# Squares of x moved ahead of two evictions, and single buffers for three of eight weight quads, in a hybrid decoder block

## The chip, the core and the metric

The kernel runs on one core of one Trainium2 chip. The metric is the time of one execution on the device in microseconds. The work is spread over TensorE (PE, the matmuls), VectorE (DVE), ScalarE (ACT), GpSimd (POOL) and SyncE (SP, which only issues DMAs here); ACT and POOL issue DMAs too. Each engine works through its own queue in order.

## The reference

One decoder layer on x of 512 tokens by 2048 channels, in float32. What matters here:

```python
u = _rmsnorm(h, norm_w)                       # h is x
proj = jnp.matmul(u, w_in)                    # 2048 x 20528
# split: mLSTM q, k, v, o, z, i, f; DeltaNet q, k, v, z, b, a; gate_a, gate_b
h_a = ... # mLSTM in chunks, per-head RMSNorm, * sigmoid(o) * silu(z)
h_b = ... # conv + silu on q, k, v, gated delta rule in chunks, RMSNorm, * silu(z)
y = sigmoid(gate_a) * (h_a @ w_out[:2048]) + sigmoid(gate_b) * (h_b @ w_out[2048:])
out = _rmsnorm(h + y, final_norm_w)
```

with `_rmsnorm(x, w) = x * rsqrt(mean(x*x) + 1e-6) * w`.

## The kernel before

**Split products.** Every large matmul is done in a reduced format in three passes. Each operand is split into a rounded part, which ACT casts (`split_hi`, L141), and the rest, which DVE subtracts (`split_lo`, L144). The passes are high by high, low by high and high by low. Weights come from DRAM through SP into `wr` tiles (4 buffers), are split into `wh` and `wl` tiles (4 buffers each, pool `wp`), and are then used by PE.

**Order of the work.** PE's order is the program's. All other engines are ordered when the program is built, by a scheduler that walks a simulated timeline and takes, on each engine, the ready instruction of the highest priority. `high_priority(offset=n)` and `urgent(level)` raise a priority (`urgent(3)` by three times `PRIO`, the weight preparation by two times), and `issue_after` puts an instruction behind a named one on its engine. On the chip each engine then keeps that order, and an instruction that has to wait holds all that stand behind it.

**The first block.** `u` is held transposed in 16 column tiles of 128 channels (k tiles, `KT` = 16), high part `uh` and low part `ul`. The load of x is in six pieces `xts[0..5]` (L270), four of 256 columns and two of 512; between them four weight tiles are loaded (`load_raw`, after pieces 0, 1, 3 and 5). The first product (`proj_cm(ML_Q, before=first_block, after=rescale)`) starts before the token factors of the norm are known:

- `make_u(kt)` turns a k tile of x with four PE transposes (L332) into PSUM; ACT writes `uh` (L333) and DVE writes `ul` (L334). These are the evictions. `first_block(kt)` calls `make_u(kt + 2)`, and two k tiles' products follow each two calls.
- The first eight k tiles (`KU` = 8) are not yet scaled by the token factor. The factor needs the sums of squares of all 2048 columns: `squares(n)` (ACT L300 for two of the four token groups, DVE L296 for the other two) for n = 0 to 5, of which 4 and 5 are the two wide pieces, called at kt = 5.
- `token_factors()` adds the sums (L303, L304), and POOL takes the power -0.5 (L305). Then `scale_x(4)`, `factor_row()` (`diag`, L318) and `scale_x(5)` follow, which scale the last 1024 columns of x before they are turned (L311, L313).
- At kt = 6 (`KU - KP`) PE multiplies ones by `diag` (`turn_row`, L324), and ACT copies the result to `rrow` (L325), the row of factors. `rescale` multiplies the half-done products by it (L396), and `scale_u` repairs the first eight k tiles of u (L341, L342).

**The seven-product blocks.** 13 blocks of the input projection (L630 to L632, `seven`) and two of the output projection compute a 512 by 1024 result by seven products of half size instead of eight. A block has a first part A of eight weight quads with four products each (m6, m1, m5, m7) and a second part B of eight quads with three products each (m1, m5, m7). B goes on in the PSUM banks of A's m1, m5 and m7; so before B's first product on a bank DVE must have added what A left there (`add`, L684, at `urgent(3)`) to `U1` or `C22`.

A quad is three weight tiles in one `wr3` tile (3 buffers). For a quad of part A, DVE computes a pair of differences (L572) and one sum `ts` (L573), and POOL stores `ts` to DRAM (L586). For a quad of part B the third tile is that stored `ts` (`t_d`, in the output blocks `t2o_d`), and DVE computes `ts = r0 - r2` (L590), which is split into single buffers `wh`, `wl`; the other two tiles, the pair, are split in one go into the wide buffers `w2h`, `w2l` (128x1024, two buffers each). Part A takes two singles and one wide buffer for each quad, part B one single and one wide buffer. `prep_sums(n + 1)` and `prep_pair(n + 1)` prepare the next quad while quad n is multiplied, `load_quad` then asks for one three ahead. All this preparation is at twice `PRIO`.

Of the kernel before, what the change touches and what calls it, by code (L numbers as in the profile page):

```python
# [8 lines left out]
F32 = mybir.dt.float32  # L9
F32R = mybir.dt.float32r  # L10
AF = mybir.ActivationFunctionType
ALU = mybir.AluOpType
# [9 lines left out]
KP = 2  # L22
# [7 lines left out]
KU = 8  # L30
HP = S // 2
KH = KT // 2
# [27 lines left out]
def hybrid_body(  # L60
# [18 lines left out]
    V, A, G, T = nc.vector, nc.scalar, nc.gpsimd, nc.tensor  # L79
# [22 lines left out]
    normc = cp.tile([P, 33], F32, tag="normc", name="normc")  # L102
# [9 lines left out]
    def load_params(tp):  # L112
        nr = tp.tile([17, P], F32, tag="prow2", name="nrow2")
        nc.sync.dma_start(nr[0:16, :], ml_norm_w.rearrange("(a p) -> a p", p=P))
        nc.sync.dma_start(nr[16:17, :], dn_norm_w.rearrange("(a p) -> a p", p=P))
        cv = dn_conv_w.rearrange("j (a p) -> (j a) p", p=P)
        crs = []
        for i in range(2):
            cr = tp.tile([96, P], F32, tag="crow", name=f"crow{i}", bufs=2)
            nc.sync.dma_start(cr, cv[i * 96:(i + 1) * 96, :])  # L120
            crs.append(cr)
        o = 0
        for ap, n in ((ml_i_bias, MLH), (ml_f_bias, MLH), (dn_a_log, DNH), (dn_dt_bias, DNH)):
            nc.sync.dma_start(bia[:, o:o + n], ap.partition_broadcast(P))
            o += n
        return crs, nr

    def turn_taps(crs, nr, psp):
        pt = psp.tile([P, 256], F32, tag="wk", name="pprt")
        T.transpose(pt[:, 192:209], nr, ident[0:17, 0:17])  # L130
        for i in range(2):
            T.transpose(pt[:, 96 * i:96 * i + 96], crs[i], ident[0:96, 0:96])
        V.tensor_scalar(out=convc, in0=pt[:, 0:192], scalar1=0.5, scalar2=None, op0=ALU.mult)
        V.tensor_scalar(out=normc[:, 16:32], in0=pt[:, 192:208], scalar1=0.125, scalar2=None, op0=ALU.mult)
        V.tensor_scalar(out=normc[:, 32:33], in0=pt[:, 208:209], scalar1=0.25, scalar2=None, op0=ALU.mult)
# [4 lines left out]
    def split_hi(hi, src):  # L140
        newest["A"] = A.copy(hi, src).ins  # L141

    def split_lo(lo, src, hi):
        newest["V"] = V.tensor_tensor(out=lo, in0=src, in1=hi.bitcast(F32), op=ALU.subtract).ins  # L144
# [20 lines left out]
    def load_raw():  # L165
        kind, c, k = plan[len(raws)]
        if kind == "i":
            src, nk, n = w_in[k * P:(k + KP) * P, c:c + NB], KP, NB
        else:
            src, nk, n = w_out[k * P:(k + 1) * P, c:c + NO], 1, NO  # L170
        with tc.high_priority(offset=2 * PRIO if len(raws) > RAHEAD else 0):
            raw = wp.tile([P, nk, n], F32, tag="wr", name="wr", bufs=NRAW)
            newest["S"] = nc.sync.dma_start(raw, src.rearrange("(k p) n -> p k n", p=P)).ins
        raws.append((raw, nk, n))
# [24 lines left out]
    def urgent(level=1):  # L199
        return tc.high_priority(offset=level * PRIO)  # L200
# [25 lines left out]
    uh = up.tile([P, KT, S], F32R, tag="uh", name="uh")  # L226
    ul = up.tile([P, KT * S + 120], F32R, tag="ul", name="ul")[:, 0:KT * S].rearrange("p (k s) -> p k s", s=S)
# [37 lines left out]
    XW = [NB] * (KU // KP) + [2 * NB] * ((KT - KU) // (2 * KP))  # L265
    xts, xat = [], []
    for n, w in enumerate(XW):
        xt = p0.tile([P, NC, w], F32, tag=f"x{n}", name=f"xt{n}")
        o = sum(XW[:n])
        nc.sync.dma_start(xt, xv[:, :, o:o + w])  # L270
        xts.append(xt)
        xat += [(xt, a) for a in range(0, w, P)]
        if n in (0, 1, 3, 5):
            load_raw()
    wg = p0.tile([P, KT, 48], F32, tag="wg", name="wg")
    wgp = p0.tile([P, KT, 112], F32R, tag="wgp", name="wgp")
# [7 lines left out]
    ss = p0.tile([P, NC, len(XW)], F32, tag="ss", name="ss")  # L284
# [1 line left out]
    rrow = p0.tile([P, S], F32, tag="rrow", name="rrow")  # L286
    half = cp.tile([P, 2, NC], F32, tag="half", name="half")
    G.memset(half, 0.5)
    done = {}

    def squares(n):
        w = XW[n]
        for c in range(NC):
            if c % 2:
                jv = p0.tile([P, 2 * NB], F32, tag="jv", name="jv")
                V.scalar_tensor_tensor(out=jv[:, 0:w], in0=xts[n][:, c, :], scalar=1.0, in1=xts[n][:, c, :], op0=ALU.mult,  # L296
                                       op1=ALU.mult, accum_out=ss[:, c, n:n + 1])
            else:
                jk = p0.tile([P, 2 * NB], F32, tag="jk", name="jk")
                A.activation(jk[:, 0:w], xts[n][:, c, :], AF.Square, accum_out=ss[:, c, n:n + 1])  # L300

    def token_factors():
        V.reduce_sum(out=rs, in_=ss, axis=mybir.AxisListType.X)  # L303
        V.tensor_scalar(out=rs, in0=rs, scalar1=1.0 / D, scalar2=EPS, op0=ALU.mult, op1=ALU.add)  # L304
        G.tensor_tensor(out=rs, in0=rs, in1=mhalf, op=ALU.pow)  # L305

    def scale_x(n):
        for c in range(NC):
            xc = xts[n][:, c, :]
            if c % 2:  # L310
                V.tensor_scalar(out=xc, in0=xc, scalar1=rs[:, c:c + 1], scalar2=None, op0=ALU.mult)  # L311
            else:
                A.mul(xc, xc, rs[:, c:c + 1])  # L313

    def factor_row():
        diag = p0.tile([P, NC, P], F32, tag="diag", name="diag")
        for c in range(NC):
            V.tensor_scalar(out=diag[:, c, :], in0=ident, scalar1=rs[:, c:c + 1], scalar2=None, op0=ALU.mult)  # L318
        return diag

    def turn_row(diag):
        pr = psj.tile([P, S], F32, tag="pj", name="prow")
        for c in range(NC):
            T.matmul(pr[:, c * P:(c + 1) * P], ones, diag[:, c, :], start=True, stop=True)  # L324
        A.copy(rrow, pr)  # L325

    def make_u(kt):
        pool, tg = ((psw, "wk"), (pso, "o"))[kt % 2]
        pt = pool.tile([P, S], F32, tag=tg, name="put")
        xt, a = xat[kt]  # L330
        for c in range(NC):
            T.transpose(pt[:, c * P:(c + 1) * P], xt[:, c, a:a + P], ident)  # L332
        done["A"] = A.activation(uh[:, kt, :], pt, AF.Copy, scale=normc[:, kt:kt + 1]).ins  # L333
        done["V"] = V.scalar_tensor_tensor(out=ul[:, kt, :], in0=pt, scalar=normc[:, kt:kt + 1],  # L334
                                           in1=uh[:, kt, :].bitcast(F32), op0=ALU.mult, op1=ALU.subtract).ins

    def scale_u(kt):
        uf = p0.tile([P, KP, S], F32, tag="uf", name="uf", bufs=2)
# [10 lines left out]
    for kt in range(UA):  # L349
        make_u(kt)  # L350
    squares(0)
    gps = {}
# [9 lines left out]
    def first_block(kt):  # L362
        if kt == 3:
            nc.sync.dma_start(wg[:, :, 0:16], w_in[:, ML_I:ML_I + 16].rearrange("(k p) n -> p k n", p=P))
            nc.sync.dma_start(wg[:, :, 16:48], w_in[:, DN_B:DN_B + 32].rearrange("(k p) n -> p k n", p=P))
        if kt == 5:
            taps.extend(load_params(p0))
        if kt == 8:
            with tc.issue_after(done["A"]):
                split_hi(wgh, wg)  # L370
            with tc.issue_after(done["V"]):
                split_lo(wgl, wg, wgh)
        if kt == 12:
            turn_taps(*taps, psw)
        if kt == KU - KP:
            turn_row(gps["diag"])
        if kt + UA < KT:
            make_u(kt + UA)
        if kt % KP and kt < 6:
            squares((kt + 1) // KP)  # L380
        if kt == 5:
            squares(4)
            squares(5)
            token_factors()
            scale_x(4)
            gps["diag"] = factor_row()
            scale_x(5)
        if kt >= KU + 1 and kt % KP:
            scale_u(kt - KU - 1)
        if kt >= KU + GLAG:  # L390
            gate_products(kt - KU - GLAG)
# [141 lines left out]
    def seven_stage(sbp, su, s4, X, t2_d, w_, k0, blocks, sinks, hook, queue):  # L533
# [4 lines left out]
        quads = [(kind, c1, c2, b, g, i) for b, (kind, c1, c2) in enumerate(blocks)  # L538
                 for g in "AB" for i in range(KH)]
# [20 lines left out]
        def split(src, wide):  # L560
            if wide:
                hi, lo = (sbp.tile([P, 2, NO], F32R, tag=f"w2{n}", name=f"w{n}", bufs=2) for n in "hl")
            else:
                hi, lo = (wp.tile([P, 1, NO], F32R, tag=f"w{n}", name=f"w{n}", bufs=NSPL) for n in "hl")
            split_hi(hi, src)
            split_lo(lo, src, hi)
            return [(hi[:, n, :], lo[:, n, :]) for n in range(2 if wide else 1)]
# [25 lines left out]
        def prep_pair(q):  # L593
            if q < len(quads):
                p_, pair = partq[q]
                with tc.high_priority(offset=2 * PRIO):
                    w2 = split(pair, True)
                partq[q] = p_ + w2 if quads[q][4] == "A" else w2 + p_

        JW, OO = ((psj, "pj"), (psw, "wk")), ((pso, "o"),) * 2  # L600
# [1217 lines left out]
```

## Time and profile before

| | before |
|---|---|
| median of three runs | 2182.06 us (2180.47 to 2186.43) |
| the profiled execution | 2178.64 us, of which the span is 2176.4 us |
| mean granted TensorE clock | 0.995 |
| DMA traffic | 444.20 MB, mean 204 GB/s |

The span runs from the first to the last instruction of the program; the time of an execution holds about 2 us more. In the profile's lines an instruction is named by its engine, its line in the kernel, its operation, and `out<-in`; where a wait stands in brackets, it gives the idle time of the engine just before the instruction and what ended it. `PEq`, `SPq` and the like are the engines' sequencers, which issue DMAs. A row of the stretches' table gives for each engine the busy time and the number of instructions, then the granted clock, the share of the DMA engines and GB/s.

### The profile page before, as it was taken

Reading aid. Unit: us, or ns where it says so; the run is one execution under the profiler, and the core shown is the slowest. Engines: PE = TensorE matmul, PEld = TensorE weight load, DVE = VectorE, ACT = ScalarE, POOL = GpSimd, SP = SyncE. Lnnn points to the kernel's source line nnn. Section 1 sums busy time; section 2 is a strip of 40 time slices with the busy share of each in tenths; the row PEclk is TensorE's granted clock in tenths of the full one; section 3 lists DMA queues with packets and bytes.
Section 4 is the critical chain, followed back from the end, with each engine's and each line's share of the span. In section 5 each row is a group of like instructions: output and inputs, shape, how many; then the busy total and the mean of one; then the engine's idle time right before and its main releaser. Section 6 shows DMA issues by size and latency. Waiting matters only on the chain. (4 is left out here: it accounts for less than half of the span.)

```text
span 2176.4 us, 31987 instructions
## 1 busy us (share of the span) xinstructions
PE 2139.7 (98%) x10552; PEld 1763.3 (81%) x10552; DVE 1726.9 (79%) x3001; ACT 1039.2 (48%) x2015; POOL 430.4 (20%) x649
## 2 busy tenths in 40 slices
PE   8999999999999999999999999999999999999998
PEld 6888888878788887888878888888888888877876
DVE  7888798888788778777756887887787888568787
ACT  5444444444444444444445545556455554344345
POOL 0000000000004000000003335235233253242211
PEclk9999999999999999999999999999999999999999
DMA  5456676667568766766867767677687678687885
GB/s 165 122 182 202 193 212 201 216 193 230 188 220 252 237 193 219 242 203 208 266 189 177 189 175 190 160 179 196 174 215 175 161 189 216 197 242 245 248 278 228
DMA packets 449159, 444.20 MB, mean 204 GB/s; under 512 B 197089, under 2 KB 305858, under 8 KB 448866
## 3 DMA queue, kind: packets, MB, share of 16 engines
q1 hardware_dynamic: 379634, 337.22, 53.9%
q0 software_dynamic: 24752, 72.90, 11.0%
q10 hardware_dynamic: 44608, 32.06, 4.7%
q8 instruction: 82, 1.34, 0.3%
q14 instruction: 83, 0.68, 0.1%
HBM read 348.66 MB, written 97.58 MB: 205 GB/s over the span
## 5 line engine op out<-in xcount | busy, mean ns | idle before, releaser
L141 ACT CAST wh<-wr 128x512 fp32r<-128x512 f32 (+1 forms) x522 | 373.3, 716 | 418.8 <-PE pj L252 226.2
L144 DVE TENSOR_TENSOR wl<-wr,wh 128x512 fp32r<-128x512 f32 (+1 forms) x522 | 435.5, 837 | 99.5 <-ACT wh L141 97.2
L251 PE MATMUL pj<-uh,wh 128*128 128x512 f32 x896 | 376.8, 421 | 0.6 <-DVE pj L396 0.5
L253 PE MATMUL pj<-uh,wl 128*128 128x512 f32 x896 | 351.4, 392 | 0.6 <-DVE wl L144 0.6
L252 PE MATMUL pj<-ul,wh 128*128 128x512 f32 x896 | 350.7, 391 | 0.0
L630 PE MATMUL ps<-wh,uh 128*128 128x512 f32 x752 | 295.1, 392 | 8.1 <-DVE X L684 7.6
L631 PE MATMUL ps<-wl,uh 128*128 128x512 f32 x752 | 295.5, 393 | 3.5 <-DVE wl L144 3.2
L632 PE MATMUL ps<-wh,ul 128*128 128x512 f32 x752 | 293.7, 391 | 0.0
L141 ACT CAST wh<-ts 128x512 fp32r<-128x512 f32 x240 | 148.1, 617 | 247.6 <-DVE ts L590 184.4
L141 ACT CAST wh<-t 128x1024 fp32r<-128x1024 f32 x120 | 126.4, 1053 | 276.3 <-PE ps L632 151.6
L630 PE MATMUL ps<-wh,suh 128*128 128x512 f32 x624 | 243.1, 390 | 1.5 <-ACT to L695 1.4
L631 PE MATMUL ps<-wl,suh 128*128 128x512 f32 x624 | 242.8, 389 | 0.0
L632 PE MATMUL ps<-wh,sul 128*128 128x512 f32 x624 | 242.8, 389 | 0.0
L586 POOL DMA_DIRECT2D t_d<-ts x104 | 56.7, 545 | 938.6 <-DVE ts L573 887.5
L253 PEld LDWEIGHTS pj<-uh,wl 128*128 128x128 f32 x896 | 168.4, 188 | 38.5 <-DVE wl L144 1.2
L251 PEld LDWEIGHTS pj<-uh,wh 128*128 128x128 f32 x896 | 169.5, 189 | 31.4 <-DVE pj L396 1.0
L252 PEld LDWEIGHTS pj<-ul,wh 128*128 128x128 f32 x896 | 169.5, 189 | 28.2
L144 DVE TENSOR_TENSOR wl<-ts,wh 128x512 fp32r<-128x512 f32 x240 | 164.0, 686 | 35.5 <-ACT wh L141 35.5
L144 DVE TENSOR_TENSOR wl<-t,wh 128x1024 fp32r<-128x1024 f32 x120 | 146.9, 1224 | 56.5 <-ACT wh L141 55.9
L630 PEld LDWEIGHTS ps<-wh,uh 128*128 128x128 f32 x752 | 141.8, 189 | 42.4 <-DVE X L684 11.8
L631 PEld LDWEIGHTS ps<-wl,uh 128*128 128x128 f32 x752 | 141.9, 189 | 39.0 <-DVE wl L144 10.4
L632 PEld LDWEIGHTS ps<-wh,ul 128*128 128x128 f32 x752 | 141.7, 188 | 28.9
(344 smaller groups left out, 3800.8 us busy)
## 6 DMA issues: line engine op xcount, KB each, us to landing
wr<-in_w_in_dram SPq DMA_DIRECT2D x744, 256.0 KB, 3.7
wr<-in_w_out_dram SPq DMA_DIRECT2D x138, 256.0 KB, 4.9
t_d<-ts POOLq DMA_DIRECT2D x104, 256.0 KB, 4.1
wr<-t_d SPq DMA_DIRECT2D x104, 256.0 KB, 3.9
tg_d<-X ACTq DMA_DIRECT2D x16, 256.0 KB, 6.6
tg_d<-to ACTq DMA_DIRECT2D x16, 256.0 KB, 6.5
v<-v_d SPq DMA_DIRECT2D x8, 512.0 KB, 5.7
mg<-g_d SPq DMA_DIRECT2D x16, 256.0 KB, 4.0
```

What stands on the lines that cost most here:

```text
L141: newest["A"] = A.copy(hi, src).ins
L144: newest["V"] = V.tensor_tensor(out=lo, in0=src, in1=hi.bitcast(F32), op=ALU.subtract).ins
L251: T.matmul(ps[j], hi[:, k, wsl], uh[:, kt, :], start=(kt == 0), stop=False, skip_group_check=after is not None)
L252: T.matmul(ps[j], hi[:, k, wsl], ul[:, kt, :], start=False, stop=False, skip_group_check=after is not None)
L253: T.matmul(ps[j], lo[:, k, wsl], uh[:, kt, :], start=False, stop=(kt == KT - 1 or (after is not None and kt == KU - 1)), skip_group_check= ...
L586: queue.dma_start(t2_d[b % 2, i], ts[:, 0, :])
L630: T.matmul(ps[t], ah, hi, start=(g == "A" and i == 0), stop=False, skip_group_check=True)
L631: T.matmul(ps[t], ah, lo, start=False, stop=False, skip_group_check=True)
L632: T.matmul(ps[t], al, hi, start=False, stop=(i == KH - 1), skip_group_check=True)
```

## The change

There are two edits.

The first is in the first block. The third weight load moves behind x's fifth piece. The squares of pieces 3, 4 and 5 are called at kt = 4, at `urgent(3)`, and before `make_u(6)`; the two evictions of k tile 6 are tied behind the last square on their engine, and those of k tile 7 follow them. The token factors, `scale_x` and `factor_row` at kt = 5 also run at `urgent(3)`.

The second is in `prep_pair`. In part B the pairs of quads 1, 3 and 5 (odd and below `KH - 1` = 7) are split tile by tile into the single buffers `wh`, `wl`, two casts and two subtractions of 128x512 instead of one each of 128x1024. Quads 0, 2, 4, 6 and 7 keep the wide buffers.

```diff
-        if n in (0, 1, 3, 5):
+        if n in (0, 1, 4, 5):
             load_raw()
...
-    done = {}
+    sq, done = {}, {}
...
     def squares(n):
...
-                V.scalar_tensor_tensor(out=jv[:, 0:w], ...)
+                sq["V"] = V.scalar_tensor_tensor(out=jv[:, 0:w], ...).ins
...
-                A.activation(jk[:, 0:w], xts[n][:, c, :], AF.Square, accum_out=ss[:, c, n:n + 1])
+                sq["A"] = A.activation(jk[:, 0:w], xts[n][:, c, :], AF.Square, accum_out=ss[:, c, n:n + 1]).ins
...
     def make_u(kt):
...
-        done["A"] = A.activation(uh[:, kt, :], pt, AF.Copy, scale=normc[:, kt:kt + 1]).ins
-        done["V"] = V.scalar_tensor_tensor(out=ul[:, kt, :], ...).ins
+        with tc.issue_after(sq["A"]) if kt == KU - KP else ExitStack():
+            done["A"] = A.activation(uh[:, kt, :], pt, AF.Copy, scale=normc[:, kt:kt + 1]).ins
+        with tc.issue_after(sq["V"]) if kt == KU - KP else ExitStack():
+            done["V"] = V.scalar_tensor_tensor(out=ul[:, kt, :], ...).ins
...
     def first_block(kt):
...
+        if kt == KU - 2 * KP:
+            with urgent(3):
+                for n in range(3, len(XW)):
+                    squares(n)
         if kt + UA < KT:
             make_u(kt + UA)
-        if kt % KP and kt < 6:
+        if kt % KP and kt < 4:
             squares((kt + 1) // KP)
         if kt == 5:
-            squares(4)
-            squares(5)
-            token_factors()
-            scale_x(4)
-            gps["diag"] = factor_row()
-            scale_x(5)
+            with urgent(3):
+                token_factors()
+                scale_x(4)
+                gps["diag"] = factor_row()
+                scale_x(5)
...
         def prep_pair(q):
             if q < len(quads):
                 p_, pair = partq[q]
+                _, _, _, _, g, i = quads[q]
                 with tc.high_priority(offset=2 * PRIO):
-                    w2 = split(pair, True)
+                    if g == "B" and i % 2 and i < KH - 1:
+                        w2 = split(pair[:, 0:1, :], False) + split(pair[:, 1:2, :], False)
+                    else:
+                        w2 = split(pair, True)
                 partq[q] = p_ + w2 if quads[q][4] == "A" else w2 + p_
```

More of the change, by code (lines that the diff above doesn't have):

```diff
@@ L295, in squares @@
                 jv = p0.tile([P, 2 * NB], F32, tag="jv", name="jv")
-                V.scalar_tensor_tensor(out=jv[:, 0:w], in0=xts[n][:, c, :], scalar=1.0, in1=xts[n][:, c, :], op0=ALU.mult,
-                                       op1=ALU.mult, accum_out=ss[:, c, n:n + 1])
+                sq["V"] = V.scalar_tensor_tensor(out=jv[:, 0:w], in0=xts[n][:, c, :], scalar=1.0, in1=xts[n][:, c, :], op0=ALU.mult,
+                                                 op1=ALU.mult, accum_out=ss[:, c, n:n + 1]).ins
             else:
                 jk = p0.tile([P, 2 * NB], F32, tag="jk", name="jk")
-                A.activation(jk[:, 0:w], xts[n][:, c, :], AF.Square, accum_out=ss[:, c, n:n + 1])
+                sq["A"] = A.activation(jk[:, 0:w], xts[n][:, c, :], AF.Square, accum_out=ss[:, c, n:n + 1]).ins
     def token_factors():
@@ L332, in make_u @@
             T.transpose(pt[:, c * P:(c + 1) * P], xt[:, c, a:a + P], ident)
-        done["A"] = A.activation(uh[:, kt, :], pt, AF.Copy, scale=normc[:, kt:kt + 1]).ins
-        done["V"] = V.scalar_tensor_tensor(out=ul[:, kt, :], in0=pt, scalar=normc[:, kt:kt + 1],
-                                           in1=uh[:, kt, :].bitcast(F32), op0=ALU.mult, op1=ALU.subtract).ins
+        with tc.issue_after(sq["A"]) if kt == KU - KP else ExitStack():
+            done["A"] = A.activation(uh[:, kt, :], pt, AF.Copy, scale=normc[:, kt:kt + 1]).ins
+        with tc.issue_after(sq["V"]) if kt == KU - KP else ExitStack():
+            done["V"] = V.scalar_tensor_tensor(out=ul[:, kt, :], in0=pt, scalar=normc[:, kt:kt + 1],
+                                               in1=uh[:, kt, :].bitcast(F32), op0=ALU.mult, op1=ALU.subtract).ins
     def scale_u(kt):
```

## The prediction

> **What bounds the kernel now.** I read the page first, then the list of waits of PE, then the stretches around each wait, then the timeline there.
>
> ```profile
> span 2176.4 us, 31987 instructions
> PE 2139.7 (98%) x10552; PEld 1763.3 (81%) x10552; DVE 1726.9 (79%) x3001; ACT 1039.2 (48%) x2015; POOL 430.4 (20%) x649
> ```
>
> PE is busy for all but 36.7 us of the span. A change that leaves the matmuls alone, as this one does, can only gain from those microseconds and from stretches in which the busy PE runs slowly. The waits of PE say who holds it (total, times, longest, in us):
>
> ```profile
> PE ps L630 <- DVE X L684: 7.6, 8, 1.8
> PE prow L324 <- DVE diag L318: 3.5, 1, 3.5
> PE ps L631 <- DVE wl L144: 3.2, 5, 1.0
> ```
>
> The second line is the wait that the first edit aims at, the first and third are those that the second edit can reach: B's first products waiting for DVE's `add`, and products waiting for a late low part. The stretches show what such a wait costs beyond itself (columns: PE, PEld, DVE, ACT, POOL busy and counts, granted clock, DMA share, GB/s):
>
> ```profile
> 19.69:23.10 3.41, 0.49 (x3) 0.07 (x1) 2.15 (x8) 1.08 (x2) 1.03 (x1) 0.99 0.55 119
> 23.10:26.51 3.41, 2.86 (x13) 2.86 (x14) 2.58 (x9) 3.12 (x6) 0.00 (x0) 0.50 0.52 134
> 26.51:29.93 3.42, 3.42 (x12) 2.84 (x11) 1.72 (x3) 2.15 (x4) 0.00 (x0) 0.51 0.81 259
> 555.49:558.90 3.41, 1.61 (x7) 1.05 (x6) 2.60 (x5) 1.57 (x2) 0.00 (x0) 1.00 0.27 88
> 558.90:562.32 3.42, 3.42 (x10) 2.64 (x9) 3.42 (x6) 1.47 (x2) 0.00 (x0) 0.51 0.01 2
> 2006.20:2009.60 3.40, 1.88 (x9) 1.47 (x9) 3.13 (x6) 1.57 (x2) 0.00 (x0) 1.00 0.44 159
> 2091.50:2094.90 3.40, 3.40 (x9) 2.66 (x9) 3.40 (x6) 1.93 (x3) 0.00 (x0) 0.50 0.10 36
> ```
>
> A stretch of 3.4 us with PE busy for 0.49 or 1.61 us is followed by one at half clock; one with 1.88 us busy kept the full clock. So a wait of about 1.7 us that falls inside one such stretch costs another 1.7 us, half of the next 3.4; the long one cost two stretches at half clock.
>
> **First edit: the squares.** The timeline of the first block, from the wait's causes to where it ends:
>
> ```profile
> 16.41 1.03 PE L332 MATMUL put<-ident,xt 128*128 128x128 f32 x8
> 17.20 0.48 PE L251 MATMUL pj<-uh,wh 128*128 128x512 f32 x1
> 17.77 0.75 DVE L334 SCALAR_TENSOR_TENSOR ul<-put,normc,uh 128x512 fp32r<-128x512 f32 x1 [0.88 <-ACT uh L333]
> 18.44 0.68 DVE L296 SCALAR_TENSOR_TENSOR jv<-xt 128x512 f32<-128x512 f32 x1
> ...
> 20.32 0.09 DVE L296 DVE_READ_ACCUMULATOR jv<-xt 128x1 f32 x1
> 20.32 0.69 DVE L144 TENSOR_TENSOR wl<-wr,wh 128x512 fp32r<-128x512 f32 x1
> 20.92 0.17 DVE L303 TENSOR_REDUCE rs<-ss 128x4 f32<-128x24 f32 x1
> 22.52 0.88 DVE L311 TENSOR_SCALAR xt<-xt,rs 128x512 f32<-128x512 f32 x2 [1.22 <-POOL rs L305]
> 23.65 2.07 PE L324 MATMUL prow<-diag,ones 128*128 128x128 f32 x8 [3.47 <-DVE diag L318]
> 25.52 1.91 PE L332 MATMUL put<-ident,xt 128*128 128x128 f32 x8
> ```
>
> The last piece of x bounds how early the squares can be. Its own load, a weight's cast, and the rate at which x and the weights come in (last number, GB/s):
>
> ```profile
> L270 SPq DMA_DIRECT2D xt<-in_x_dram x1: 2169/2169/2169, 6.1 to 6.1; - x1
> DMA to landing us min/median/max: 11.0/11.0/11.0
> 11.95 0.63 ACT L141 CAST wh<-wr 128x512 fp32r<-128x512 f32 x1
> 10.00:15.00 5.00, 4.62 (x24) 3.94 (x25) 4.74 (x13) 4.40 (x12) 0.00 (x0) 1.00 1.06 405
> ```
>
> It lands at 6.1 + 11.0 = 17.1, and the change puts the same bytes ahead of it, so that stays. DVE then spent 17.77 to 20.41 on two squares with two evictions between them, and one weight's low part before the sum.
>
> 1. With the evictions behind, the two squares follow the landing: 17.1 + 2 x (0.68 + 0.08) = 18.6 instead of 20.4. The 0.08 is the reading of the sum that follows each square. ACT's two squares end alike.
> 2. At `urgent(3)` the sum no longer stands behind the low part at 20.32. From the sum's start to the first `prow` it took 23.65 - 20.92 = 2.73, which the change keeps: 18.6 + 2.7 = 21.3. PE is free at 23.65 - 3.47 = 20.18, so 3.5 of waiting becomes 1.2: minus 2.3 us.
> 3. The two evictions on DVE, 0.75 each, fall into the 1.22 that DVE idles while POOL takes the power; the rest, 0.3, may push `diag`. PE needs those two k tiles only after `prow` and the next transposes, so nothing else waits; without that cover 1.5 would come onto the chain, which is more than half of the gain.
> 4. 1.2 idle leaves PE busy for 2.2 of its 3.4 us, more than the 1.88 that kept the clock. So the half clock goes. PE was busy 2.86 + 3.42 = 6.28 us at half clock; eight transposes took 1.03 at full and 1.91 at half, a ratio of 1.85, so 6.28 x (1 - 1/1.85) = minus 2.9 us.
> 5. The load order: the fourth and fifth pieces of x move ahead of a weight of 256 KB, which is 0.6 us at 405 GB/s for the fifth alone; the weight comes 1 MB later, 2.6 us, so its cast at 11.95 moves to about 14.6 and its low part, 0.63 + 0.69 later, to 15.9. PE first uses it at 17.20. Cost nothing, with 1.3 us of cover; beyond it PE waits one for one.
>
> What is given back shows in the next rows:
>
> ```profile
> 27.77 0.62 ACT L141 CAST wh<-wr 128x512 fp32r<-128x512 f32 x1 [1.40 <-DMA wr<-in_w_in_dram]
> 28.30 0.58 ACT L325 COPY rrow<-prow 128x512 f32<-128x512 f32 x1
> 28.43 0.69 DVE L144 TENSOR_TENSOR wl<-wr,wh 128x512 fp32r<-128x512 f32 x1 [1.32 <-ACT wh L141]
> 30.83 0.69 DVE L396 TENSOR_TENSOR pj<-pj,rrow 128x512 f32<-128x512 f32 x1
> 30.00:35.00 5.00, 4.47 (x24) 3.43 (x24) 5.00 (x8) 2.66 (x5) 0.00 (x0) 1.00 0.21 56
> 45.00:50.00 5.00, 5.00 (x23) 3.73 (x22) 5.00 (x7) 1.69 (x3) 0.00 (x0) 1.00 0.14 43
> ```
>
> From 30 to 50 us DVE has no idle time (these are the first and last of four stretches); its repair of u ends the first block. The 5.2 us reach the end only if DVE's work starts as much earlier. About two low parts that DVE now does while it idles, such as that at 28.43, would come into its full stretch: 2 x 0.6 = 1.2. First edit: 2.3 + 2.9 - 1.2 = minus 4.0 us, between minus 5.2 and, if the chain moves to ACT (below), about minus 0.8.
>
> **Second edit: the quads.** Part B of each block on DVE and ACT, and the longest wait:
>
> ```profile
> L144 DVE TENSOR_TENSOR wl<-ts,wh 128x512 fp32r<-128x512 f32 x240 | 164.0, 686 | 35.5 <-ACT wh L141 35.5
> L144 DVE TENSOR_TENSOR wl<-wr,wh 128x1024 fp32r<-128x1024 f32 x120 | 146.0, 1222 | 19.6 <-ACT wh L141 19.5
> L590 DVE TENSOR_TENSOR ts<-wr 128x512 f32<-128x512 f32 x120 | 82.9, 691 | 101.5 <-DMA wr<-t_d 78.2 <-DMA wr<-t2o_d 17.2 <-issue 5.2
> 556.30 0.69 DVE L590 TENSOR_TENSOR ts<-wr 128x512 f32<-128x512 f32 x1 [3.56 <-DMA wr<-t_d]
> 556.90 1.88 DVE L684 TENSOR_TENSOR X<-X,ps 128x512 f32<-128x512 f32 x3
> 557.64 0.50 PE L630 MATMUL ps<-wh,uh 128*128 128x512 f32 x1 [1.79 <-DVE X L684]
> ```
>
> The 120 wide low parts of part B are 15 blocks of 8, so three of eight are 45 quads. Each gives 2 x 0.686 - 1.222 = 0.15 us more on DVE, 6.7 us in all. That lies beside DVE's 101.5 us of idle time before `ts` in the same parts, and I cost it at nothing; with no cover it would be 6.7. ACT, at 48%, has more room.
>
> What it moves is buffers. The first odd pair of B needed the wide buffer of A's last quad, free after that quad's fourth product; now it needs the two singles of that quad, free after its first and second. So it can be split during A's last quad. That also frees its `wr3` tile sooner for a later load.
>
> In the rows, DVE stood at `ts` for a DMA from before 553 to 556.30, with three adds behind it, though they outrank it: the scheduler had found `ts` ready first in its own time. The two new subtractions come ahead of that `ts` in the program at the same priority, and may fill that place until the adds are ready. Then a wait of 8 goes, or shrinks to what is left for B's next bank. I take half of 7.6, 3.8, and one of the two half clocks at 558.90 and 2091.50, 1.7. Against it stand new waits of the third kind in the list, 0.64 each by 3.2 in 5: three of them, 2.0. Second edit: 3.8 + 1.7 - 2.0 = minus 3.5 us; ends minus 11.0 (all of 7.6 and both half clocks) and plus 6.7 (the added DVE time in full). I take a value near the middle, leaning to the waits that have a row.
>
> Sum: 4.0 + 3.5 = minus 7.5 us. The profiled execution took 2178.64, 2.2 of it outside the span; it would take 2171.1. It stood 3.4 below the median of 2182.06, which I take as the base: 2174.6 us.
>
> The Trainium skill bears on the clock: "TensorE: Matmul & The Clock Gate", section "Part 1: The HAM clock gate", has PE fall to half rate after at least one idle window of about 3.4 us. By it the waits in the blocks would have cost no half clock, and the sum would be 7.5 - 1.7 = minus 5.8; the trace disagrees, since 1.61 us busy of 3.41 was enough for it.
>
> **The rivals.**
>
> *ACT takes the chain.* At 27.77 a weight's cast waited for its DMA, and `rrow` and the next evictions stood behind it. The load's time is set by SP's queue and hardly moves. If that cast stays in front, DVE's rescale at 30.83 stays within 0.8, and the sum is 0.8 + 3.5 = minus 4.3: 2177.8. For it: the order stands in the trace. Against: the load waits for the buffer of the third weight, which comes 2.6 later, while `rrow` is ready 2.3 earlier, so their order should turn.
>
> *The quads move nothing.* DVE's loads come as before and the same `ts` stands before the adds. Minus 4.0: 2178.1. For it: the second quad's load waits for A's last tile, which no edit touches.
>
> *Slower: the singles run out.* The `ts` of B's first two quads and the new pair fill all four; the third `ts` must wait for B's first quad to end. Its cast stands in ACT's queue, with copies of PSUM behind it, for which PE waits as it did once:
>
> ```profile
> PE ps L630 <- ACT to L695: 1.4, 1, 1.4
> ```
>
> At 1.0 in each of 15 blocks it is 15 - 4.0 = plus 11: 2193. It makes the kernel slower by over 0.3% from 0.7 in each block on. Against: that `ts` is used only two quads later.
>
> *Half clocks that don't come from these waits.* Then 5.8: 2176.3.
>
> *The change does not do what it says:* the scheduler finds other work first, and both waits stay: 2181.5.
>
> **How the numbers follow.** Forecast 0.44, ACT 0.16, quads 0.19, slower 0.13, half clocks 0.04, nothing 0.04. About 0.3% or 6.5 us is what a measurement of this kernel can tell from no change. The forecast's own range is 2168 to 2178, and some three quarters of it lie below 2175.5: 0.34; from the ends of the other gains comes 0.09, so faster is 0.43. Slower is the 0.13 and a little of the rest, 0.15; same 0.42. The range is 2168 to 2185: below it lie a tenth (all 11.0 of the second edit), above it the slower rival.
>
> **What would show it.** `prow` after a wait of 1.2 rather than 3.5, at about 21.3, and full clock in 23.10 to 29.93; `rrow` before the cast that waits for its DMA; 45 fewer low parts of 128x1024; fewer than 7.6 us under "ps L630 <- DVE X L684". The forecast is wrong if `prow` starts after 22.5, if the end of the first block moves less than 3 us, or if new waits on `wh` or `wl` in the blocks pass 5 us.

## The result, and the profile after

| | before | after |
|---|---|---|
| median | 2182.8 us (2176.82 to 2186.43, 6 runs) | 2194.11 us (2189.96 to 2199.15, 6 runs) |
| ratio | 1 | 1.0057, 95% interval 1.0037 to 1.0077 |
| the profiled execution, its span | 2178.64, 2176.4 | 2193.5, 2191.7 |

The change makes the kernel slower by 11.3 us by the medians, 12 by the ratio. Lines of the program carry other numbers in each kernel: in the changed one the add is L693, part B's `ts` L595, the seven-product matmuls L639 to L641, the evictions L334 and L336, the rescaling L401; in the runs below they lie a few lines off. The head of the page:

```profile
span 2191.7 us, 32049 instructions
PE 2139.0 (98%) x10552; PEld 1759.8 (80%) x10552; DVE 1726.9 (79%) x3046; ACT 1051.6 (48%) x2060; POOL 429.5 (20%) x649
```

PE's busy time fell by 0.7 us, and its idle time rose from 36.7 to 2191.7 - 2139.0 = 52.7 us: 16.0 more. The list of the waits of PE (in all, times, longest) says where:

```profile
PE ps L639 <- DVE X L693: 24.5, 23, 3.1
PE prow L324 <- DVE diag L318: 3.9, 1, 3.9
PE ps L640 <- DVE wl L144: 3.5, 6, 1.2
```

The wait for the add went from 7.6 us in 8 to 24.5 in 23; that is 16.9 more, about as much as PE's whole added idle time of 16.0. The wait for `prow`, which the first edit was to cut to 1.2, is 0.4 longer. The two edits are read apart.

**The first block after.** DVE's timeline, and PE's:

```profile
18.35 0.75 DVE L336 SCALAR_TENSOR_TENSOR ul<-put,normc,uh 128x512 fp32r<-128x512 f32 x1 [0.82 <-ACT uh L334]
19.01 0.68 DVE L296 SCALAR_TENSOR_TENSOR jv<-xt 128x512 f32<-128x512 f32 x1
...
20.36 0.08 DVE L296 DVE_READ_ACCUMULATOR jv<-xt 128x1 f32 x1
20.36 0.68 DVE L144 TENSOR_TENSOR wl<-wr,wh 128x512 fp32r<-128x512 f32 x1
20.96 0.17 DVE L303 TENSOR_REDUCE rs<-ss 128x4 f32<-128x24 f32 x1
21.05 0.74 DVE L336 SCALAR_TENSOR_TENSOR ul<-put,normc,uh 128x512 fp32r<-128x512 f32 x1
21.70 0.16 DVE L304 TENSOR_SCALAR rs<-rs 128x4 f32<-128x4 f32 x1
23.09 0.88 DVE L311 TENSOR_SCALAR xt<-xt,rs 128x512 f32<-128x512 f32 x2 [1.23 <-POOL rs L305]
```
```profile
24.22 2.08 PE L324 MATMUL prow<-diag,ones 128*128 128x128 f32 x8 [3.90 <-DVE diag L318]
```

Only k tile 6's evictions are tied behind the squares. (The text on the change above says that tile 7's follow them; the diff has no tie for tile 7.) So tile 7's eviction stands ahead of the last two squares, at 18.35, and keeps them until 19.01. They end at 20.44, where they ended at 20.41 before. A weight's low part still stands ahead of the sum. And tile 6's eviction, set free by the last square, got in between the sum L303 and its scaling L304, which adds about 0.5.

**A turn from part A to part B, before and after.** DVE's timeline of the same block, first of the kernel before:

```profile
938.58 1.23 DVE L144 TENSOR_TENSOR wl<-wr,wh 128x1024 fp32r<-128x1024 f32 x1 [1.16 <-ACT wh L141]
939.72 0.68 DVE L684 TENSOR_TENSOR X<-X,ps 128x512 f32<-128x512 f32 x1
941.14 0.69 DVE L590 TENSOR_TENSOR ts<-wr 128x512 f32<-128x512 f32 x1 [0.74 <-issue]
941.75 1.88 DVE L684 TENSOR_TENSOR X<-X,ps 128x512 f32<-128x512 f32 x3
943.54 0.69 DVE L144 TENSOR_TENSOR wl<-ts,wh 128x512 fp32r<-128x512 f32 x1
944.14 1.28 DVE L684 TENSOR_TENSOR X<-X,ps 128x512 f32<-128x512 f32 x2
945.34 0.69 DVE L590 TENSOR_TENSOR ts<-wr 128x512 f32<-128x512 f32 x1
945.94 2.36 DVE L144 TENSOR_TENSOR wl<-wr,wh 128x1024 fp32r<-128x1024 f32 x2
```

and of the kernel after, with PE's product that follows:

```profile
951.56 0.68 DVE L693 TENSOR_TENSOR X<-X,ps 128x512 f32<-128x512 f32 x1
952.86 0.69 DVE L595 TENSOR_TENSOR ts<-wr 128x512 f32<-128x512 f32 x1 [0.63 <-issue]
953.47 0.68 DVE L144 TENSOR_TENSOR wl<-wr,wh 128x512 fp32r<-128x512 f32 x1
954.07 1.27 DVE L693 TENSOR_TENSOR X<-X,ps 128x512 f32<-128x512 f32 x2
955.27 0.68 DVE L144 TENSOR_TENSOR wl<-wr,wh 128x512 fp32r<-128x512 f32 x1
955.87 1.28 DVE L693 TENSOR_TENSOR X<-X,ps 128x512 f32<-128x512 f32 x2
957.07 0.68 DVE L595 TENSOR_TENSOR ts<-wr 128x512 f32<-128x512 f32 x1
957.67 1.22 DVE L144 TENSOR_TENSOR wl<-wr,wh 128x1024 fp32r<-128x1024 f32 x1
958.80 0.68 DVE L693 TENSOR_TENSOR X<-X,ps 128x512 f32<-128x512 f32 x1
```
```profile
959.53 0.50 PE L639 MATMUL ps<-wh,uh 128*128 128x512 f32 x1 [1.28 <-DVE X L693]
```

Six additions (1 + 3 + 2, and 1 + 2 + 2 + 1) let PE go on in the banks. Before, one `ts` and one low part stood between them, and from the first to the end of the last it took 945.42 - 939.72 = 5.70 us. After, five instructions stand between them: quad 2's `ts`, the two single low parts of quad 1's pair, quad 3's `ts`, and quad 2's wide low part. It takes 959.48 - 951.56 = 7.92 us, and PE waits 1.28. Over the 15 blocks, the median of this stretch went from 5.53 to 7.77 us.

### The profile page after: what moved, and what is told of

Read it like the earlier page. It is cut to its first block, busy times and chain, and to the rows that moved or that the text cites. A ratio compares the mean times of both kernels' runs of the same rounds, so it can differ in the third digit from the quotient of the medians.

```text
span 2191.7 us, 32049 instructions
## 1 busy us (share of the span) xinstructions
PE 2139.0 (98%) x10552; PEld 1759.8 (80%) x10552; DVE 1726.9 (79%) x3046; ACT 1051.6 (48%) x2060; POOL 429.5 (20%) x649
## 5 line engine op out<-in xcount | busy, mean ns | idle before, releaser
L141 ACT CAST wh<-wr 128x512 fp32r<-128x512 f32 (+1 forms) x567 | 382.2, 676 | 548.7 <-PE pj L252 223.5
L144 DVE TENSOR_TENSOR wl<-wr,wh 128x512 fp32r<-128x512 f32 (+1 forms) x567 | 444.5, 786 | 97.0 <-ACT wh L141 91.4
L639 PE MATMUL ps<-wh,uh 128*128 128x512 f32 x752 | 296.0, 394 | 23.3 <-DVE X L693 23.0
L641 PE MATMUL ps<-wh,ul 128*128 128x512 f32 x752 | 293.3, 390 | 0.0
L639 PE MATMUL ps<-wh,suh 128*128 128x512 f32 x624 | 242.7, 389 | 0.0
L641 PE MATMUL ps<-wh,sul 128*128 128x512 f32 x624 | 242.7, 389 | 0.0
L639 PEld LDWEIGHTS ps<-wh,uh 128*128 128x128 f32 x752 | 141.4, 188 | 62.8 <-DVE X L693 33.7
L595 DVE TENSOR_TENSOR ts<-wr 128x512 f32<-128x512 f32 x120 | 82.8, 690 | 125.4 <-DMA wr<-t_d 96.4
```

The source lines that it names most:

```text
L595: V.tensor_tensor(out=ts[:, 0, :], in0=r[:, 0, :], in1=r[:, 2, :], op=ALU.subtract)
L639: T.matmul(ps[t], ah, hi, start=(g == "A" and i == 0), stop=False, skip_group_check=True)
L641: T.matmul(ps[t], al, hi, start=False, stop=(i == KH - 1), skip_group_check=True)
```

## The experiments

**Theory.** The loss is an order on DVE. Single buffers for quad 1's pair free a wide buffer, so quad 2's pair can be split earlier, in the scheduler's time before the last addition is ready. DVE then does it ahead of that addition, though the addition outranks it. The first edit brings nothing, for the order on DVE and ACT in the first block. **Rivals:** the four singles run out and preparation waits for PE; the added work on DVE (45 quads, 0.15 us each) costs its 6.7; the first edit is at fault.

The first four runs stand beside a kernel before of 2177.8 us.

### Each edit alone, and quads of the second edit alone

The edit of the first run is the diff above without `prep_pair`; that of the second is `prep_pair` alone. The other two narrow its condition:

```diff
-                    if g == "B" and i % 2 and i < KH - 1:
+                    if g == "B" and i in (3, 5):      # third run
+                    if g == "B" and i == 1:           # fourth run
```

First edit alone. 

> The first edit alone. In the changed kernel's trace the first block ends 0.1 us later than before, and the wait ahead of prow is 3.9 instead of 3.5, because k tile 7's evictions, which carry no tie, went ahead of the last squares. Theory (the loss is all in the quads): 2183, within 3 of before. Rival (the first edit shifts the planner's clock and so disorders later stages): 5 or more above before.

Measured 2177.87 us, ratio 0.9997 (0.9982 to 1.0012): no change.

Second edit alone. 

> The second edit alone. Theory (the loss is all in the quads, about 1 us at each of 15 changes from part A to part B): 12 to 16 above before, about 2196, with some 24 us of PE waiting for the adds. Rival (the two edits only hurt together): within 4 of before.

Measured 2200.49 us, ratio 1.0102 (1.0065 to 1.0140): 22.7 more, the theory's sign, but about 7 more than its upper end. The first edit is not at fault. (With it, in the whole change, the ratio was 1.0057, up to 1.0077; the intervals overlap, and the two were not measured side by side, so that the second edit loses more alone isn't shown.)

Quads 3 and 5 alone. 

> The second edit for quads 3 and 5 only; quad 1 keeps the wide buffer. Theory (only quad 1's singles put other work of DVE among the adds at the change from A to B): DVE's order there is as before, so 2183, within 3 of before. Rival one (the four singles run out wherever a pair uses them): two thirds of the loss, plus 9. Rival two (the added 0.15 us of DVE for each quad): 30 quads, plus 4.5.

Measured 2175.04 us, ratio 0.9983 (0.9969 to 0.9998): no loss. Two thirds of the added DVE work are in it, so that work has its cover; and a pair in a ring of four singles does no harm by itself.

Quad 1 alone. 

> The second edit for quad 1 only. Theory (its singles fill DVE's order among the adds and free the wide buffer, so that quad 2's pair comes ahead of the last add): the whole loss, plus 12 to 16, with 15 quads instead of 45. Rival one (singles run out, equally at each pair): a third, plus 5. Rival two (added DVE work): plus 2.

Measured 2190.96 us, ratio 1.0062 (1.0043 to 1.0080): 13.2 more. PE's waits for the addition in the second, third and fourth run:

```profile
PE ps L634 <- DVE X L688: 24.3, 26, 2.0
```
```profile
PE ps L634 <- DVE X L688: 6.6, 6, 3.1
```
```profile
PE ps L634 <- DVE X L688: 22.2, 22, 1.9
```

The waits come with quad 1, and with it alone, as the theory has it. All three quads together measured 9.5 us more than quad 1 alone. Whether quads 3 and 5 add that when quad 1 is there stays open: the two intervals overlap, the second run has four times only, and the waits differ by 2.1 us.

### The order of DVE alone

The next two keep the second edit's buffers, and hold DVE's work back by a tie behind the last of the six additions. In one it is only quad 2's wide low part:

```diff
-                    w2 = split(pair, True)
+                    with tc.issue_after(newest["add"]) if g == "B" and i == 2 else ExitStack():
+                        w2 = split(pair, True)
...
-            V.tensor_tensor(out=x, in0=a, in1=b, op=ALU.add)
+            newest["add"] = V.tensor_tensor(out=x, in0=a, in1=b, op=ALU.add).ins
```

> The second edit alone, with the low part of quad 2's pair held behind the last of the six additions; the four single buffers are as full as in the second edit alone (2200.5 us against 2177.8 for the kernel before). Theory (the loss is what VectorE does ahead of the last addition: 3.6 us in the second edit, 1.8 us in the kernel before): 2.4 us stand ahead of the last addition here, 0.6 more than before where 1.8 more made waits of about 1.0 to 1.3; so the waits of TensorE for an addition at the block's turn fall from 24 us to under 10, and the time to 2178 to 2188. Rival (the four singles run out, so that preparation waits for TensorE): the buffers are used as before this change of order, so the time stays at 2195 to 2201 and the waits are for a weight's low part.

Measured 2177.87 us against 2177.82, ratio 0.9998 (0.9988 to 1.0008). One tie takes away the whole loss of the second edit, the 9.5 us that were open too, with the buffers unchanged. PE's wait for the additions, and DVE's timeline at the turn:

```profile
PE ps L635 <- DVE X L689: 12.4, 14, 3.9
```
```profile
949.37 0.69 DVE L590 TENSOR_TENSOR ts<-wr 128x512 f32<-128x512 f32 x1
949.98 0.68 DVE L689 TENSOR_TENSOR X<-X,ps 128x512 f32<-128x512 f32 x1
950.57 1.22 DVE L144 TENSOR_TENSOR wl<-wr,wh 128x1024 fp32r<-128x1024 f32 x1
```

The wide low part stands behind the last addition. The median stretch from the first to the last addition is 6.66 us here, 1.1 longer than before. In seven of the 15 blocks it is 6.6 to 7.4 us and PE waits for no addition; in the changed kernel the same seven take 7.7 to 8.0, and PE waits 1.2 to 1.3 in each. So in these blocks the additions had about 1 us of slack, and the wide low part, 1.22, is what passed it. In the other eight blocks waits stay: 12.4 us in all, half of the second edit's 24.3, but more than the 7.6 of before and than the 10 that was expected at most. The time is that of before all the same, and so, nearly, is PE's whole idle time in the profiles, 38.9 us against 36.7. The rival with the singles falls too: they are as full here. (A ring of more than four singles was not tried.)

In the other all six additions stand first: quad 2's and quad 3's `ts` and the low parts of the pairs of quads 1 to 3 are tied behind the last.

```diff
+                    with tc.issue_after(newest["add"]) if i in (2, 3) else ExitStack():
                         V.tensor_tensor(out=ts[:, 0, :], in0=r[:, 0, :], in1=r[:, 2, :], op=ALU.subtract)
...
+                    with tc.issue_after(newest["add"]) if g == "B" and i in (1, 2, 3) else ExitStack():
                         # the two ways to split the pair, as in the change
```

> The second edit alone, with the subtractions of quads 2 and 3 of part B and the pairs' low parts of quads 1 to 3 held behind the last of the six additions: the additions stand first. Theory (order on VectorE): waits of TensorE for an addition fall below the 6.6 us of the kernel before, to under 3; time 2168 to 2180, unless the preparation that now comes later makes waits for a weight's low part, which would be seen by name. Rival (singles run out): 2190 to 2201, with waits for a low part. Rival (the second edit's loss beyond quad 1, 9.5 us, has a cause of its own in quads 3 and 5 together with quad 1): 2182 to 2190.

Measured 2166.26 us, ratio 0.9944 (0.9929 to 0.9960): 11.6 less than the kernel before, and below the range that was expected. The last kernel of this group has neither edit, only the kernel before with quad 2's `ts` tied behind the last addition (`if i == 2`):

> The kernel before, with only the subtraction of quad 2 of part B (and with it what reads it) held behind the last of the six additions. Theory: the kernel before's waits for an addition (6.6 to 7.6 us) and the half clocks that follow some of them go: 4 to 11 us less than the kernel before, 2167 to 2174. Rival: the additions have slack in nearly every block and the later preparation makes waits of its own: within 3 us of the kernel before, or slower, with waits for a low part in the place of those for an addition.

Measured 2165.76 us, ratio 0.9949 (0.9931 to 0.9967), again a little below the expected range. The waits of PE in both, first the second edit's buffers, then those of before, and DVE's timeline of the latter:

```profile
PE ps L637 <- DVE wl L144: 8.6, 10, 2.2
```
```profile
PE ps L632 <- DVE wl L144: 6.2, 5, 2.1
```
```profile
932.40 3.90 DVE L685 TENSOR_TENSOR X<-X,ps 128x512 f32<-128x512 f32 x6
936.22 0.69 DVE L591 TENSOR_TENSOR ts<-wr 128x512 f32<-128x512 f32 x1
```

No wait for one of the six additions is left in either list. (One of 1.5 us for `X` stands in both; it is for the output projection's own line.) In their place stand waits for a low part, 8.6 and 6.2 us; those were 3.2 before. The kernel is faster all the same: in this profile PE idled 2163.3 - 2131.8 = 31.5 us against 36.7, and was busy 7.9 less (the page's PE has 2131.8). Behind the first block and ahead of the tail PE ran at half clock for three stretches of 3.4 us before (from 558.95, 1955.00 and 2091.53) and for one here (from 2081.56). Two fewer are about 3 of the 7.9, by the prediction's ratio of 1.85; the rest is open. The gain that the second edit was meant to bring lay in the order, and needs none of its buffers.

### The first block's two orders

Both last k tiles' evictions are tied behind the last squares:

```diff
-        with tc.issue_after(sq["A"]) if kt == KU - KP else ExitStack():
+        with tc.issue_after(sq["A"]) if kt in (KU - KP, KU - KP + 1) else ExitStack():
...
-        with tc.issue_after(sq["V"]) if kt == KU - KP else ExitStack():
+        with tc.issue_after(sq["V"]) if kt in (KU - KP, KU - KP + 1) else ExitStack():
```

> The first edit alone, with the evictions of both last k tiles held behind the last squares on ScalarE and on VectorE; ScalarE's order behind that is left as it is, with the cast that waits for its transfer ahead of the row's copy. Theory (two faults in a row: VectorE's order makes TensorE wait for the row's products, ScalarE's order keeps the row itself): TensorE's wait for the products falls to about 1.7 us as in the run that mended both, but the row's copy stays at about 28 us, the wait for the rescaling grows instead, to 2 or 3 us, and the time is within 2 us of the first edit alone, 2176 to 2178. Rival (the evictions' place alone was the fault): 2172 to 2175, as with both mended.

Measured 2176.36 us against 2178.69, ratio 1.0000 (0.9985 to 1.0015). PE's waits and ACT's timeline:

```profile
PE pj L251 <- DVE pj L401: 4.5, 1, 4.5
...
PE prow L324 <- DVE diag L318: 1.8, 1, 1.8
```
```profile
28.08 0.62 ACT L141 CAST wh<-wr 128x512 fp32r<-128x512 f32 x1 [2.05 <-DMA wr<-in_w_in_dram]
28.60 0.58 ACT L325 COPY rrow<-prow 128x512 f32<-128x512 f32 x1
29.08 1.27 ACT L334 ACTIVATE uh<-put,normc 128x512 fp32r<-128x512 f32 x2
```

The wait for `prow` fell from 3.9 to 1.8, and all of it and more came back: the wait for the rescaling L401, which reads `rrow`, is 4.5, where it was 1.3 after the change and 2 to 3 was expected. ACT copies `rrow` at 28.60, behind a cast that waits for its DMA, as before (28.30). So the first half of the chain is not the bound. The next run, on top of this one, holds that cast back as well:

```diff
-        while len(parts) < min(limit[0], i + SAHEAD + 1):
+        while len(parts) < min(limit[0], i + SAHEAD + (i != HOLD)):   # HOLD = 3
...
-            split_hi(hi, raw)
-            split_lo(lo, raw, hi)
+            late = len(parts) in (HOLD + SAHEAD, HOLD + SAHEAD + 1)
+            with tc.issue_after(done["A"]) if late else ExitStack():
+                split_hi(hi, raw)
+            with tc.issue_after(done["R"]) if late else ExitStack():   # the second rescaling
+                split_lo(lo, raw, hi)
```

> The first edit alone, with the evictions of both last k tiles held behind the last squares, and with one weight cast, which waits for its data, held behind the evictions of k tile 9 on ScalarE (its low part behind the second rescaling on VectorE). Theory (the first edit brought nothing because tile 7's eviction stayed ahead of the squares, tile 6's got between the sum and its scaling, and ScalarE's copy of the row stood behind a cast that waits for a transfer): TensorE's wait for the row's products falls from 3.9 us to about 1.5 to 2, the copy of the row starts at about 26.5 us instead of 28.4, the wait for the rescaling (1.3 us) goes; 3 to 6 us less than the first edit alone, so 2172 to 2175 where that gave 2177.9. Rival (another transfer or the later cast bounds the first block anyway): within 1.5 us of the first edit alone, with a new wait of the same size behind it in the first 45 us.

Measured 2174.19 us against 2177.82, ratio 0.9981 (0.9970 to 0.9992). PE's and ACT's timelines:

```profile
23.80 1.16 PE L330 MATMUL prow<-diag,ones 128*128 128x128 f32 x8 [1.70 <-DVE diag L324]
24.80 1.04 PE L338 MATMUL put<-ident,xt 128*128 128x128 f32 x8
...
32.09 0.50 PE L257 MATMUL pj<-uh,wh 128*128 128x512 f32 x1 [0.88 <-DVE pj L407]
```
```profile
26.22 0.58 ACT L331 COPY rrow<-prow 128x512 f32<-128x512 f32 x1
26.69 1.27 ACT L340 ACTIVATE uh<-put,normc 128x512 fp32r<-128x512 f32 x2
27.84 0.63 ACT L142 CAST wh<-wr 128x512 fp32r<-128x512 f32 x1
```

The row is copied 2.2 us earlier than after the change (28.43), PE waits 1.70 and 0.88, and the eight transposes behind `prow` take 1.04, so the clock is full. The median is 3.6 less. This is about what the first edit was to be worth.

### Both mended together

The first block as in the last run, with three versions of the blocks: the change's buffers and additions first (11.6 alone); the buffers of before and quad 2's `ts` behind the additions; the same with quads 3 and 5 in singles.

> The whole change with its two orders mended: both evictions behind the squares and one cast later, as in the run that measured 2174.2 us; the additions first and the preparation of quads 1 to 3 behind them, as in the run that measured 2166.3 us; the kernel before measured 2177.8 beside both. Theory (the two places are independent): the gains of 3.6 and 11.6 us add up, 2161 to 2165. Rival (the gain of the first block is given back later, in a wait that is hidden anyway): 2165 to 2168.

> The kernel before's buffers, no single buffers for any pair, with the two orders mended: the first block as in the run of 2174.2 us, and quad 2's subtraction behind the last addition as in the run of 2165.8 us. Theory (the gain comes from the order, not from the single buffers): 2160 to 2165, the same as or below the mended change. Rival (the buffers are worth something once the order is mended): over 2 us above the mended change.

> As the run with the two orders mended and the kernel before's buffers, and with quads 3 and 5 of part B in single buffers. Theory (single buffers for these two let quad 4's and quad 6's pairs be prepared earlier, worth 0 to 3 us, 2.7 measured with the kernel before's order): 0 to 4 us below the run without them, 2157 to 2164. Rival (that gain came from the same waits that the order has taken away, or more subtractions in narrower instructions cost VectorE time): the same time or up to 3 us above it.

Measured, beside 2178.69 for the kernel before: 2163.51 us, ratio 0.9930 (0.9913 to 0.9947); 2164.86, 0.9934 (0.9916 to 0.9951); 2163.60, 0.9927 (0.9912 to 0.9943). The gains add up: 0.9944 x 0.9981 = 0.9925 and 0.9949 x 0.9981 = 0.9930. The three can't be told from one another, so the single buffers are worth nothing that these runs can show. All three beat both kernels, by some 14 to 15 us and, by the ratios, 1.3% against the changed one.

## Why the prediction was wrong

The forecast was 2174.6 us, 7.5 less; the kernel takes 11.3 more by the medians.

**Second edit, the step that failed.** "The two new subtractions come ahead of that `ts` … and may fill that place until the adds are ready. Then a wait of 8 goes". The place was taken to be idle time ahead of the additions. The rows show that quad 1's subtractions stand between the additions, `ts` stays ahead of them, and one more piece of work is set free that the prediction did not follow: the freed wide buffer lets quad 2's pair go ahead of the last addition. Predicted minus 3.5; measured plus 22.7 alone. Held behind the addition by one tie, the edit measured the same as the kernel before. That it is the freed buffer which lets the pair go ahead is read from the program and from quad 1's run, in which the buffers alone differ; no run shows the scheduler's own times.

The term under it was of the right size, but not the edit's to collect: the lower end, minus 11.0 for all of the 7.6 of waiting and both half clocks, is about what the additions measured when put first (11.6 and 12.1 less). In part that is luck: in the profile of the latter, PE's idle time is 5.2 us less and its busy time 7.9 less, where the term had 7.6 and 3.4. That more waits on `wl` would come was right for those runs, but 2.0 (by its own working 3 x 0.64 = 1.9) was too little: 5.4 and 3.0; in the change itself it is 0.3. And 1.7 us of half clock behind a wait of 1.7 us was a chance and not a sure price, as the last section shows.

**The added DVE work at nothing.** Held: the wide low parts of `wr` fell from 120 to 75 and quads 3 and 5, two thirds of the 6.7, showed no loss.

**First edit, steps 1 and 2.** "The two squares follow the landing" and "the sum no longer stands behind the low part": both failed. Tile 7's eviction has no tie and went ahead of the squares, the low part stayed ahead of the sum, and the wait grew from 3.5 to 3.9. Urgency did not move the sum. Alone the edit measured no change, where minus 4.0 was forecast.

**Step 3.** That both evictions fall into DVE's idle time during the power: tile 6's did not, it stands ahead of L304, which starts the power. With both tied, one fell there and the other stood behind `diag`; the wait was then 1.8, 1.7 less than the kernel before's 3.5, where 2.3 less was forecast.

**Step 4.** After the change the half clock stayed; the stretches:

```profile
19.40:22.81 3.41, 0.92 (x5) 0.42 (x3) 2.43 (x8) 1.38 (x4) 0.79 (x1) 1.00 0.68 145
22.81:26.22 3.41, 2.00 (x9) 2.00 (x10) 3.06 (x9) 2.96 (x5) 0.24 (x1) 0.50 0.45 97
26.22:29.63 3.41, 3.41 (x14) 3.02 (x13) 1.39 (x2) 2.35 (x6) 0.00 (x0) 0.50 0.88 266
```

With the wait at 1.70 the clock was full behind it, as the step had it. Over all profiles: with this wait at 1.4 to 1.8 us (five) no half clock follows it; at 3.5 to 3.9 (nine) six have two stretches of it, two have one, and one has none. So the 2.9 was a likely term, not a sure one. **Step 5** held in its result: the weight that was moved back was not waited for. But its cast came at 16.11 instead of 14.6 and its low part was done at 17.53 instead of 15.9; PE first used that part at 17.89, so the cover was about 0.4 us, not 1.3. (Only x's fifth piece moved ahead of that weight; the fourth stood there already. The sum used the fifth's 1 MB alone.) **The give-back** was named in the rival "ACT takes the chain", and that rival is shown: with only the first half mended, `rrow` stayed behind its cast. With both halves mended the first edit measured 3.6, forecast 4.0; the totals are close, and no run measured the three parts of the 4.0 one by one.

**The slower rival.** It gave 2193, and 2194.11 was measured, but by another mechanism. It had ACT holding PE; the waits of after have no line for ACT in the blocks. The singles were as full in the run with the one tie, and that lost nothing. Its 1.0 in each of 15 blocks came near by chance: here it is DVE that makes PE wait 1.28 in the block shown.

## What to carry to other kernels

In these kernels a priority did not pull urgent work past less urgent work that stood ahead of it: by the way the scheduler is built, it orders only what is ready at the same moment of the scheduler's time. When an edit frees a buffer, list everything that the buffer lets start earlier, and ask which urgent instruction will now stand behind it in the same in-order queue. Where a few instructions gate the busiest engine, tie the rest behind them, and follow a chain through every engine that it crosses before counting on the gain of its first half.

## What the runs showed of the hardware that was not expected

The half clock does not follow from a wait's length alone. In the run with quad 1 only, the wait for `prow` was as long as in the kernel before, 3.46 against 3.47, and the eight products behind it took 1.16 us instead of 2.07:

```profile
25.09 1.16 PE L324 MATMUL prow<-diag,ones 128*128 128x128 f32 x8 [3.46 <-DVE diag L318]
```
```profile
20.15:23.56 3.41, 1.48 (x7) 0.90 (x5) 2.55 (x8) 1.45 (x5) 0.67 (x1) 1.00 0.45 109
23.56:26.97 3.41, 1.88 (x17) 1.88 (x18) 3.01 (x9) 3.01 (x6) 0.36 (x1) 1.00 0.63 160
```

PE had come free there at 25.09 - 3.46 = 21.63, in the kernel before at 20.18. The two stretches (behind the comma stands PE's busy time, third from the end the clock) are counted back in steps of 3.413 us from where this run's one half clock begins, at 2177.38, behind the last matmul. The border of two stretches lies inside the wait, and they kept 1.48 and 1.88 us of work; in the kernel before one stretch held nearly the whole wait and kept 0.49. The Trainium skill, "TensorE: Matmul & The Clock Gate", section "Part 1: The HAM clock gate", says that the window is free-running and does not start with the kernel. The traces agree: a border lies at 23.06 us from the first instruction in the kernel before, at 23.56 here and at 25.31 in the run with one tie.

Nor is there one sharp limit. Counted like that in all fourteen profiles, from 14 us to the last matmuls, every stretch at full clock in which PE was busy for 1.45 us or less of 3.41 was followed by half clock, and none with 1.88 or more; between 1.48 and 1.87 both came. The prediction's 1.61, which lost the clock, lies in that band; 1.48 kept it here. So a wait of one length came with its half clock and without it, and one profile's count of half clocks is not a sure term of a sum. No run here moved the wait alone.
